# A second block of 128 tokens per expert, computed inside the expert loop

## The chip, the cores and the metric

The kernel runs on one core of one Trainium2 chip. The metric is the device time of one execution in microseconds (us). TensorE (PE) multiplies, and its weight loads (PEld) overlap its matmuls; VectorE (DVE), ScalarE (ACT) and GpSimd (POOL) do the element work; SyncE (SP) issues most DMA transfers. Every engine works through its own instruction stream and waits for the others on semaphores.

## What the reference computes

Six 128-row tiles of tokens (256 context, 512 latent) pass a first block of two layers and a second block of two layers. Both layers of the first block end in a mixture of experts, and only this part is touched:

```python
def hier_moe(h, w_rg, b_rg, w_re, b_re, w_gate, w_up, w_down):
    ...                                  # group, then top 2 of its 8 experts: 2 experts and weights a token
    order = jnp.argsort(flat_e)          # (token, expert) pairs sorted by expert
    padded = ((counts + MOE_BLOCK - 1) // MOE_BLOCK) * MOE_BLOCK      # MOE_BLOCK = 128
    ...
    def run_block(args):
        xb, e = args
        return (jax.nn.silu(xb @ w_gate[e]) * (xb @ w_up[e])) @ w_down[e]
    ...
    return jnp.zeros((n, d), h.dtype).at[tok_sorted].add(y[dest] * w_sorted[:, None])
```

There are 32 experts a layer. gate and up are 1024 x 512, down is 512 x 1024, all fp32: 6 MB an expert. Layer 0 routes 768 tokens (1536 pairs), layer 1 routes 512 (1024 pairs). Evaluated on its inputs, the reference's router gives, in layer 0, more than 64 pairs to experts 8, 10, 11, 12, 13 and 14, and more than 128 to expert 14 alone (132). In layer 1 experts 28 (65) and 31 (83) exceed 64, and none exceeds 128.

## The kernel before, in words

`moe` runs one layer. `scores` has sorted the pairs: `tix` lists for every expert the rows of its first 128 tokens, `idx` and `wl` where their results go and by what factor. `experts` (L1332) loops over the 32 experts in Python, so the code is unrolled. In step e GpSimd gathers the tokens of expert e+2 (`ex_load`, L1260), SyncE issues the twelve 512 KB weight chunks of expert e+1 (`ex_load_w`, `wraw`, L144), and TensorE finishes gate and up for the first 64 tokens of expert e (`ex_in`, L1275), transposes the tokens of e+1 (`ex_x`, L1284) and starts expert e+1. The chunks lie in a ring of 32 buffers (4 + 28), 2 2/3 experts deep: a chunk of a later expert can be issued when the chunk that had its buffer is no longer read.

Then `ex_arms` (L1376) branches: every engine has loaded the row of token 64 into a register (`values_load`, L1359). If it is a token, `ex_rest` computes the second 64 tokens too and writes both halves out; else `ex_out` writes one half: transposes (L1308), a copy (L1309), the down product, the scaling on VectorE (L1319 in layer 0 alone, L1320) and a scatter into the DRAM table Y by GpSimd (L1321).

Behind the loop come the blocks past 128 tokens. `past` (L1181) makes their lists in three steps, `count`, `blocks` and `fill`, that run behind the steps of the first experts; the number of such blocks is the register `nov`. If `nov > 0`, the weights of the first overflow expert are loaded again (`overflow`, L1139) and `ex_block` (L1146) computes it; a loop under `nov > 1` (L1149) does any further ones. Between the loop and this block `gains` spreads rows for the next stage (L441, L442). The next stage reads Y back (`load`, L52 after inlining into the pinned section) and warms TensorE up with a few matmuls.

The order of instructions on each engine is chosen by a planner that simulates the program; what goes through `keep_in_program_order` keeps its place among such instructions. The same planner spreads DMAs over eight completion counters shared by SyncE's and ScalarE's transfers; a DMA waits until the one before it on its counter is complete, whichever engine issued it.

Of the kernel before, what the change touches and what calls it, by code (L numbers as in the profile page):

```python
# [8 lines left out]
F32 = mybir.dt.float32  # L9
F32R = mybir.dt.float32r  # L10
BF = mybir.dt.bfloat16
# [21 lines left out]
NEG = -1.0e30  # L33
NOB = 12
RING = 4
MRING = 28
# [30 lines left out]
class Ker:  # L67
# [518 lines left out]
    def mixer_ab(self, xO, begin=None):  # L586
# [8 lines left out]
        with ExitStack() as eo:  # L595
# [260 lines left out]
            with ExitStack() as e1:  # L856
                pp = e1.enter_context(self.pool(name="abp", bufs=1))
                ps = e1.enter_context(self.pool(name="abps6", bufs=3, space=PSUM))
                self.weights(e1, 8, 0, "right")
                G = []  # L860

                def loads():
                    for t in (0, 1):
                        nc.sync.dma_start(xO[:, t, :], xsrc(t))
                    G.append(self.mod_rows(pp, 0, 1, 2, "gc", eng=nc.sync))
                    G.append(self.mod_rows(pp, 0, 0, 2, "gl", eng=nc.sync))
                    for t in range(2, NT):
# [213 lines left out]
    def moe(self, l, xO, t0, nt, who_of, sc=None, then=()):  # L1081
# [12 lines left out]
        with ExitStack() as e1:  # L1094
# [5 lines left out]
            off = pw.tile([P, 1], F32, name="off")  # L1100
            ctx = None if l else pw.tile([P, 2, NE + NOB], F32, name="ctx")
            for h in range(2):
                nc.gpsimd.memset(off[h * 64:h * 64 + 64], 2 * BIG + h)
# [6 lines left out]
            px = e1.enter_context(self.pool(name=f"mx{l}", bufs=2, side="right"))  # L1110
            ps = e1.enter_context(self.pool(name=f"mqs{l}", bufs=8, space=PSUM))
            xg = [pg.tile([P, D], F32, name=f"xg{i}", tag=f"xg{i}") for i in range(3)]
# [10 lines left out]
            past = self.past(nt, sc["K"], idx, tix, wl, eid, px, ps, off, ctx)  # L1123

# [10 lines left out]
            def overflow():  # L1135
# [3 lines left out]
                with tc.If(nov > 0):  # L1139
# [3 lines left out]
                return nov, w  # L1143
            nov, w = self.experts(l, tix, idx, wl, ctx, xg, hD, Y, T, px, ps,
                                  [first] + past + ([] if l else [self.shift_scale]), gains, overflow)
            with tc.If(nov > 0):  # L1146
                self.ex_block(w, xo, slots, px, ps, nc.values_load(tix[64:65, NE:NE + 1], min_val=0, max_val=int(BIG)))
            self.n = RING + 11
            with tc.If(nov > 1):  # L1149
# [30 lines left out]

    def past(self, nt, K, idx, tix, wl, eid, px, ps, off, ctx):  # L1181

# [6 lines left out]
        t_ = {}  # L1189

        def count():
            t_["iota"], t_["tri"] = self.const("iota128", [P, P], px), self.const("tri", [P, P], px)
            tri = t_["tri"]
# [5 lines left out]
            nb, nbi = T2("nb", 1, F32, NE), T2("nbi", 1, I32, NE)  # L1199
            v.tensor_scalar(nb, cn[:NE, 0:1], float(P - 1), None, ALU.add)  # L1200
            v.tensor_copy(nbi, nb)
# [10 lines left out]
        def blocks():  # L1212
# [10 lines left out]
            v.tensor_scalar(eid[:, :NOB], ef, float(NE - 1), None, ALU.min)  # L1223
            v.tensor_copy(eid[:, NOB:NOB + 1], ov[:, 2 * NE - 1:2 * NE])
            for k in range(2):
                tmp = px.tile([P, nt, NE], F32, name="ptmp", tag="ptmp", bufs=1)
# [3 lines left out]
                hi, bl, rm, neg = (T2(f"{n}{k}", nt) for n in ("hi", "bl", "rm", "ng"))  # L1230
                v.tensor_scalar(hi, K["r"][:, k], float(-P), None, ALU.add)
                ii = T2(f"ii{k}", nt, I32)
# [14 lines left out]
        def fill():  # L1247
# [28 lines left out]

    def ex_x(self, xg, px, ps):

        x = px.tile([P, 8, P], F32, name="xT", tag="xT")
        for g in range(2):  # L1280
# [20 lines left out]
    def ex_out(self, w, sg, h, idx, wl, Y, T, px, ps):  # L1301
# [29 lines left out]

    def experts(self, l, tix, idx, wl, ctx, xg, hD, Y, T, px, ps, past, gains, overflow):  # L1332

# [4 lines left out]
        w = self.ex_load_w(l, 0)  # L1338
        a = ps.tile([P, 512], F32, name="ea", tag="b")
        self.ex_in(a, w, x, 0, range(2))  # L1340
        for e in range(NE):
            if e + 2 <= NE:
                self.ex_load(tix[:, e + 2:e + 3], xg[(e + 2) % 3], hD, T)
# [11 lines left out]
            if e + 1 < NE:  # L1355
                a = ps.tile([P, 512], F32, name="ea", tag="b")
# [8 lines left out]
    def ex_block(self, w, xg, out, px, ps, more=None):  # L1365

        x = self.ex_x(xg, px, ps)
# [30 lines left out]
    def table(self, fn):  # L1398

        t = self.sm.tile([P, 1], F32, name="tab")  # L1400
        self.nc.scalar.activation(t, self.eps[EPS], fn)
# [9 lines left out]
    def mixer_na(self, xO, begin=None, finish=None):  # L1411
# [13 lines left out]
        with ExitStack() as e1:  # L1425
# [3 lines left out]
            with ExitStack() as e2:  # L1429
# [23 lines left out]
                with ExitStack() as e3:  # L1453
# [4 lines left out]
                    with self.pinned():  # L1458
# [32 lines left out]
                        for t in range(NT + 2):  # L1491
# [245 lines left out]
    def even_mixer(self, xO, normed=False, finish=None):  # L1737
# [3 lines left out]
        with ExitStack() as e1:  # L1741
            OT = xO[:, 4:6, :].rearrange("p a (b n) -> p (a b) n", n=512)
            with ExitStack() as e2:
# [8 lines left out]
                with ExitStack() as e3:  # L1752
# [46 lines left out]
                    else:  # L1799
# [148 lines left out]
    def conv_ffn(self, l, xO, dst=None):  # L1948
        nc, tc, I = self.nc, self.tc, self.I
        wu, wd = I["ffn_w_up_2"][l], I["ffn_w_down_2"][l]  # L1950
        with ExitStack() as e1:
            ph = e1.enter_context(self.pool(name=f"ff{l}", bufs=1))
            ps = self.banks()
# [361 lines left out]
```

## Time and profile before

| what | us |
| --- | --- |
| median of 3 runs (lowest, highest) | 3520.12 (3518.69, 3525.53) |
| the profiled execution | 3519.27 |
| its span, first to last instruction | 3517.5 |
| TensorE busy in the span | 3270.0 (93%) |
| VectorE, ScalarE, GpSimd busy | 1515.1, 1027.7, 468.3 |

The expert loop of layer 0 lies at about 611 to 1172 us of the span, its overflow block at 1175 to 1193, and the loop of layer 1 at about 1644 to 2165. A busy TensorE is an engine with an instruction in it; it does not say that the rest of the kernel waits for it.

### The profile page before, as it was taken

Reading aid. Unit: us, or ns where it says so; the run is one execution under the profiler, and the core shown is the slowest. Engines: PE = TensorE matmul, PEld = TensorE weight load, DVE = VectorE, ACT = ScalarE, POOL = GpSimd, SP = SyncE. Lnnn points to the kernel's source line nnn. Section 1 sums busy time; section 2 is a strip of 40 time slices with the busy share of each in tenths; the row PEclk is TensorE's granted clock in tenths of the full one; section 3 lists DMA queues with packets and bytes.
Section 4 is the critical chain, followed back from the end, with each engine's and each line's share of the span. In section 5 each row is a group of like instructions: output and inputs, shape, how many; then the busy total and the mean of one; then the engine's idle time right before and its main releaser. Section 6 shows DMA issues by size and latency. Waiting matters only on the chain. (4 is left out here: it accounts for less than half of the span.)

```text
span 3517.5 us, 44393 instructions
## 1 busy us (share of the span) xinstructions
PE 3270.0 (93%) x16460; PEld 2118.1 (60%) x16460; DVE 1515.1 (43%) x2899; ACT 1027.7 (29%) x1908; POOL 468.3 (13%) x569
## 2 busy tenths in 40 slices
PE   7999998999988699998988888998999999999998
PEld 5954556333322387765332234876888888788887
DVE  3476565222222356565211114527443456455344
ACT  3475541100000144441000002326332334333232
POOL 1044421111111023331111110103000000000000
PEclk9999999999999899999999999999999999999999
DMA  5134465798999622236999996322333354233331
GB/s 202 49 119 133 166 217 196 306 417 329 352 410 397 229 73 75 69 113 226 416 408 399 402 397 244 122 91 85 96 96 96 84 66 95 70 99 105 96 97 48
DMA packets 350859, 676.34 MB, mean 192 GB/s; under 512 B 42804, under 2 KB 194548, under 8 KB 349184
## 3 DMA queue, kind: packets, MB, share of 16 engines
q1 hardware_dynamic: 313816, 626.50, 50.6%
q0 software_dynamic: 17360, 25.94, 2.1%
q10 hardware_dynamic: 19416, 20.34, 1.8%
q8 instruction: 168, 2.75, 0.3%
q14 instruction: 99, 0.81, 0.1%
HBM read 676.22 MB, written 29.19 MB: 201 GB/s over the span
## 5 line engine op out<-in xcount | busy, mean ns | idle before, releaser
L1275 PE MATMUL ea<-wr,xT 128*64 128x512 f32 x2336 | 607.5, 601 | 38.5 <-DMA wr<-in_moe_w_up_dram 21.8
L157 DVE TENSOR_TENSOR wh<-wr,wh 128x1024 fp32r<-128x1024 f32 (+2 forms) x269 | 328.8, 1228 | 308.9 <-ACT wh L156 308.2
L240 PE MATMUL aw<-hh,wh 128*128 128x512 f32 (+1 forms) x1184 | 432.1, 366 | 2.9 <-ACT wh L156 2.6
L241 PE MATMUL aw<-hl,wh 128*128 128x512 f32 (+1 forms) x1184 | 432.7, 366 | 0.0
L242 PE MATMUL aw<-hh,wh 128*128 128x512 f32 (+1 forms) x1184 | 431.4, 365 | 0.0
L1275 PEld LDWEIGHTS ea<-wr,xT 128*64 128x64 f32 x2336 | 178.9, 137 | 408.9 <-issue 293.5
L156 ACT CAST wh<-wr 128x1024 fp32r<-128x1024 f32 (+2 forms) x269 | 274.2, 1027 | 417.6 <-PE acc L242 287.4
L1275 PE MATMUL ea<-wr,aT 128*64 128x512 f32 x1168 | 284.4, 632 | 53.0 <-DVE aT L1309 43.5
L240 PEld LDWEIGHTS aw<-hh,wh 128*128 128x128 f32 x1184 | 223.9, 189 | 39.7 <-ACT wh L156 3.5
L241 PEld LDWEIGHTS aw<-hl,wh 128*128 128x128 f32 x1184 | 224.3, 189 | 38.3 <-issue 3.5
L242 PEld LDWEIGHTS aw<-hh,wh 128*128 128x128 f32 x1184 | 224.1, 189 | 37.6 <-issue 3.5
L510 POOL TENSOR_TENSOR pp<-pp,rc 128x768 f32<-128x768 f32 (+3 forms) x192 | 211.0, 1106 | 260.0 <-DVE rc L509 247.3
L1285 ACT COPY xT<-pt 128x512 f32<-128x512 f32 x65 | 38.1, 586 | 683.8 <-PE pt L1284 672.9
L1275 PEld LDWEIGHTS ea<-wr,aT 128*64 128x64 f32 x1168 | 82.7, 144 | 200.1 <-issue 136.6
L1321 POOL DMA_INDIRECT Y<-ey,idx x73 | 73.1, 1001 | 848.3 <-DVE ey L1320 767.2
L508 ACT ACTIVATE pp<-s,nm 128x768 f32<-128x768 f32 (+3 forms) x192 | 137.1, 716 | 157.4 <-DVE nm L1593 81.1
L240 PE MATMUL acc<-wh,hh 128*128 128x512 f32 (+2 forms) x480 | 177.8, 370 | 0.0
L241 PE MATMUL acc<-wh,hh 128*128 128x512 f32 (+2 forms) x480 | 176.4, 368 | 0.0
L242 PE MATMUL acc<-wh,hl 128*128 128x512 f32 (+2 forms) x480 | 176.1, 367 | 0.0
L1297 ACT ACTIVATE sg<-ea 64x256 f32<-64x256 f32 x146 | 54.9, 376 | 302.4 <-PE ea L1275 237.7
L241 PE MATMUL acc<-wh,ah 128*128 128x512 f32 x352 | 137.8, 392 | 0.0
L1298 DVE TENSOR_TENSOR sg<-sg,ea 64x256 f32<-64x256 f32 x146 | 62.0, 425 | 175.7 <-ACT sg L1297 173.0
(493 smaller groups left out, 5166.5 us busy)
## 6 DMA issues: line engine op xcount, KB each, us to landing
wr<-in_moe_w_gate_dram SPq DMA_DIRECT2D x260, 512.0 KB
wr<-in_moe_w_up_dram SPq DMA_DIRECT2D x260, 512.0 KB
wr<-in_moe_w_down_dram SPq DMA_DIRECT2D x260, 512.0 KB
wr<-in_w_ada_dram SPq DMA_DIRECT2D x96, 512.0 KB
wr<-in_ffn_w_up_dram SPq DMA_DIRECT2D x88, 512.0 KB
wr<-in_ffn_w_down_dram SPq DMA_DIRECT2D x44, 512.0 KB
wr<-in_odd_w_in_dram SPq DMA_DIRECT2D x32, 512.0 KB
wr<-in_na_w_in_dram SPq DMA_DIRECT2D x30, 512.0 KB
```

Source lines behind the costliest of these rows:

```text
L156: keep(self.nc.scalar.copy(hi, raw))
L157: keep((self.lo_eng or self.nc.vector).tensor_sub(lo, raw, f(hi)))
L240: mm(ps, ah, bh, start=first, stop=False)
L241: mm(ps, ah, bl, start=False, stop=False)
L242: mm(ps, al, bh, start=False, stop=last)
L508: nc.scalar.activation(p[:, :n], s[:, b:b + n], AF.Exp, bias=nm, scale=sign, accum_out=rc)
L510: nc.gpsimd.tensor_mul(p[:, :n], p[:, :n], rc.broadcast_to([P, n]))
L1275: self.tc.keep_in_program_order(self.nc.tensor.matmul(*a, **k))
L1285: (self.nc.vector.tensor_copy if g else self.nc.scalar.copy)(x[:, g * 4:g * 4 + 4, :], pt.rearrange("p (k t) -> p k t", t=P))
L1297: self.nc.scalar.activation(sg[64:, c], a[:64, c], AF.Silu)
L1298: self.nc.vector.tensor_mul(sg[64:, c], sg[64:, c], a[64:, c])
L1321: nc.gpsimd.indirect_dma_start(Y.rearrange("t (h d) -> (t h) d", h=2), bass.IndirectOffsetOnAxis(ap=idx[:, h], axis=0), y, None, bounds_ch ...
```

## The change

Experts 3 to 31 (`TWO = 3`) get a second block of up to 128 tokens in the loop, from the weights that are still loaded: behind the arms of expert e stands a branch on the first row of its second list; in it are a gather, `ex_block` with all its arms, and the scatters. A new step `second` of `past`, at expert 1, makes the lists for it; `count`, `blocks`, `fill` move one expert later and count only what exceeds 256 tokens (128 for experts 0 to 2). Both branch registers are loaded at the head of each step. `gains` moves behind the first overflow block. `ea`, the product that is started early, has two PSUM banks of its own, the rest six. L1319 keeps its program order. Two `warm` calls read another tile (one has 9 matmuls for 6), and small unused tiles (`pad`) shift SBUF addresses.

```diff
+TWO = 3
@@ mixer_ab, mixer_na, conv_ffn
+                self.pad(e1, 192, "right")
...
+                self.pad(e2, 352, "right")
...
+                self.pad(e1, 192)
@@ past
+        def second():
+            t_["iota"], t_["tri"] = self.const("iota128", [P, P], px), self.const("tri", [P, P], px)
+            so, sw = (ps.tile([P, 512], F32, name=n, tag="b")[:, :NE] for n in ("so2", "sw2"))
+            for k in range(2):
+                rm = T2(f"rm{k}", nt)
+                v.tensor_scalar(rm, K["r"][:, k], float(-P), None, ALU.add)
+                R2 = px.tile([P, nt, P], BF, name="R2", tag=f"R2{k}", bufs=1)
+                self.ranked(R2, rm, t_["iota"])
+                for acc, val in ((so, K["aid"]), (sw, K["wp"])):
+                    self.lists(acc, R2, self.marks(px, K["E"][:, k], val[:, k]), k == 0, k == 1)
+            self.places(so, two["tix"])
+            for dst, acc, o in ((two["idx"], so, off), (two["wl"], sw, None)):
+                t = T2("ovs2", NE)
+                v.tensor_copy(t, acc)
+                self.both(dst, t, ps, o, two["ctx"] if o is not None else None)
...
-        return [count, blocks, fill]
+        return [second, count, blocks, fill]
@@ ex_out
-            nc.vector.scalar_tensor_tensor(y, self.dgain, ctx[:, h], self.gain, ALU.mult, ALU.add)
+            self.tc.keep_in_program_order(
+                nc.vector.scalar_tensor_tensor(y, self.dgain, ctx[:, h], self.gain, ALU.mult, ALU.add))
@@ experts
         for e in range(NE):
+            more = nc.values_load(tix[64:65, e:e + 1], min_val=0, max_val=int(BIG))
+            if e >= TWO:
+                tok = two["tix"][:, e:e + 1]
+                more2 = nc.values_load(tok[0:1], min_val=0, max_val=int(BIG))
...
-            more = nc.values_load(tix[64:65, e:e + 1], min_val=0, max_val=int(BIG))
+
+            def second():
+                with self.tc.If(more2 < T):
+                    self.ex_load(tok, xg[e % 3], hD, T)
+                    at = [q if q is None else q[:, :, e:e + 1] for q in (two["idx"], two["wl"], two["ctx"])]
+                    self.ex_block(w, xg[e % 3], (at[0], at[1:], Y, T, px, ps), px, ps,
+                                  nc.values_load(tok[64:65], min_val=0, max_val=int(BIG)), x)
             self.ex_arms(more, w, x, sg, out, px, ps)
+            if e >= TWO:
+                second()
             w, x = w1, x1
-        gains()
@@ moe
-            ps = e1.enter_context(self.pool(name=f"mqs{l}", bufs=8, space=PSUM))
+            ps = e1.enter_context(self.pool(name=f"mqs{l}", bufs=6, space=PSUM))
...
             with tc.If(nov > 0):
                 self.ex_block(w, xo, slots, px, ps, nc.values_load(tix[64:65, NE:NE + 1], min_val=0, max_val=int(BIG)))
+            gains()
@@ mixer_na, even_mixer
-                                self.warm(ps, xO[:, 0, 0:512], 6)
+                                self.warm(ps, A[0][:, 0:512], 6)
...
-                        self.warm(ps, xO[:, 2, 0:512], 6)
+                        self.warm(ps, self.gfin[:, 0:512], 9)
```

## Rows read from the trace of the kernel before

**Rows 1.** Busy us (count) of each engine by stretch, then granted clock, DMA share, GB/s.

```profile
820.00:920.00 100.00, 94.23 (x462) 33.32 (x459) 24.59 (x45) 8.36 (x20) 12.04 (x12) 1.00 0.83 292
920.00:1150.00 230.00, 208.47 (x884) 69.64 (x882) 51.31 (x89) 20.08 (x45) 28.31 (x28) 1.00 1.02 405
1650.00:1660.00 10.00, 9.41 (x72) 4.90 (x72) 2.38 (x6) 3.21 (x5) 1.00 (x1) 1.00 0.08 14
1840.00:2130.00 290.00, 254.98 (x1066) 87.78 (x1064) 47.38 (x88) 23.51 (x53) 33.44 (x33) 0.96 1.02 401
```

**Rows 2.** What SyncE waited for, 600 to 700 us: total us, times, longest.

```profile
SPq L144 <- PE pt L1308: 21.5, 3, 15.9
SPq L144 <- DMA c_aid<-const_aid_dram: 16.2, 1, 16.2
```

**Rows 3.** The same, 820 to 920 us: all of its answer.

```profile
SPq L144 <- PE ea L1275: 62.3, 26, 9.4
SPq L144 <- PE pt L1308: 9.0, 3, 8.0
```

**Rows 4.** Timeline of TensorE: transposes for experts 15 to 17, a down product between.

```profile
882.66 1.09 PE L1284 MATMUL pt<-c_ident,xg 128*128 128x128 f32 x8
906.97 1.09 PE L1284 MATMUL pt<-c_ident,xg 128*128 128x128 f32 x8
...
915.99 3.65 PE L1275 MATMUL ea<-wr,aT 128*64 128x512 f32 x16 [0.52 <-DVE aT L1309]
...
919.58 1.09 PE L1284 MATMUL pt<-c_ident,xg 128*128 128x128 f32 x8
```

**Rows 5.** The same in layer 1, two light experts that follow each other.

```profile
1740.37 1.09 PE L1284 MATMUL pt<-c_ident,xg 128*128 128x128 f32 x8
1754.77 1.09 PE L1284 MATMUL pt<-c_ident,xg 128*128 128x128 f32 x8
```

**Rows 6.** Timeline behind expert 14's last product: VectorE's scaling, GpSimd's scatter and gather.

```profile
907.09 0.75 DVE L1320 SCALAR_TENSOR_TENSOR ey<-ea,wl,ey 128x512 f32<-128x512 f32 x1 [3.76 <-PE ea L1275]
...
908.12 0.96 POOL L1321 DMA_INDIRECT Y<-ey,idx  x1 [3.85 <-DVE ey L1320]
909.39 1.04 POOL L1260 DMA_INDIRECT xg<-hD,tix  x1 [0.30 <-issue]
```

**Rows 7.** Line L1260, all gathers of the kernel: issue to landing.

```profile
DMA to landing us min/median/max: 3.2/7.1/9.1
```

**Rows 8.** Timeline of layer 0's end: expert 31's last product, then the overflow block.

```profile
1165.32 0.75 DVE L1319 SCALAR_TENSOR_TENSOR ey<-dgain,ctx,gain 128x512 f32<-128x512 f32 x1 [5.48 <-DMA Y<-ey,idx]
...
1166.63 5.00 PE L1275 MATMUL ea<-wr,aT 128*64 128x512 f32 x16 [6.40 <-issue]
...
1171.67 0.75 DVE L1320 SCALAR_TENSOR_TENSOR ey<-ea,wl,ey 128x512 f32<-128x512 f32 x1 [5.14 <-PE ea L1275]
...
1175.33 1.09 PE L1284 MATMUL pt<-c_ident,xg 128*128 128x128 f32 x8
...
1187.11 5.00 PE L1275 MATMUL ea<-wr,aT 128*64 128x512 f32 x16 [1.17 <-DVE aT L1309]
...
1192.17 0.75 DVE L1320 SCALAR_TENSOR_TENSOR ey<-ea,wl,ey 128x512 f32<-128x512 f32 x1 [5.11 <-PE ea L1275]
```

**Rows 9.** Timeline of layer 1's end: the matmuls of `gains`, before an overflow branch not entered.

```profile
2164.26 2.05 PE L441 MATMUL mrow<-gsrc,c_ident 16*128 16x128 f32 x16
```

**Rows 10.** Sequencer instructions of three branch lines and the register load: ns min/median/max.

```profile
L1146 PEldq EVENT_SEMAPHORE  x2: 51/51/51, 2166.3 to 2166.5; - x2
L1149 PEldq COMPARE_BRANCH  x2: 329/892/1454, 1187.4 to 2166.7; - x2
L1376 PEldq COMPARE_BRANCH  x74: 70/234/3554, 625.2 to 2160.7; - x74
L1359 PEldq TENSOR_LOAD <-tix x64: 295/303/493, 624.6 to 2144.9; - x64
```

**Rows 11.** Groups by line, 590 to 700 us: list matmuls of 32 columns, rank comparison.

```profile
L1058 PE MATMUL swp<-Wm,Rm 128*128 128x32 bf16 x36 | 1.2, 176 | 0.0
L1050 DVE TENSOR_TENSOR R<-c_iota,rm 128x768 bf16<-128x768 f32 x2 | 1.9, 950 | 0.0
```

More of the change, by code (lines that the diff above doesn't have):

```diff
@@ L1101, in moe @@
             ctx = None if l else pw.tile([P, 2, NE + NOB], F32, name="ctx")
+            two = dict(tix=pw.tile([P, NE], I32, name="tix2"), idx=pw.tile([P, 2, NE], I32, name="idx2"),
+                       wl=pw.tile([P, 2, NE], F32, name="wl2"), ctx=None if l else pw.tile([P, 2, NE], F32, name="ctx2"))
             for h in range(2):
@@ L1122, in gains @@
                     self.nA = {w: self.spread(pg, self.nmod[0], 16 * w + 8, ps, f"xg{i}") for i, w in enumerate(ws)}
-            past = self.past(nt, sc["K"], idx, tix, wl, eid, px, ps, off, ctx)
+            past = self.past(nt, sc["K"], idx, tix, wl, eid, px, ps, off, ctx, two)
             def first():
@@ L1143, in overflow @@
                 return nov, w
-            nov, w = self.experts(l, tix, idx, wl, ctx, xg, hD, Y, T, px, ps,
-                                  [first] + past + ([] if l else [self.shift_scale]), gains, overflow)
+            nov, w = self.experts(l, tix, idx, wl, ctx, two, xg, hD, Y, T, px, ps,
+                                  [first] + past + ([] if l else [self.shift_scale]), overflow)
             with tc.If(nov > 0):
                 self.ex_block(w, xo, slots, px, ps, nc.values_load(tix[64:65, NE:NE + 1], min_val=0, max_val=int(BIG)))
+            gains()
             self.n = RING + 11
@@ L1179, in moe, with past @@
         return finish
-    def past(self, nt, K, idx, tix, wl, eid, px, ps, off, ctx):
+    def past(self, nt, K, idx, tix, wl, eid, px, ps, off, ctx, two):
         nc = self.nc
@@ L1189, in past @@
         t_ = {}
+        def second():
[13 more added lines that the diff above has]
+                self.both(dst, t, ps, o, two["ctx"] if o is not None else None)
         def count():
-            t_["iota"], t_["tri"] = self.const("iota128", [P, P], px), self.const("tri", [P, P], px)
             tri = t_["tri"]
@@ L1199, in count @@
             nb, nbi = T2("nb", 1, F32, NE), T2("nbi", 1, I32, NE)
-            v.tensor_scalar(nb, cn[:NE, 0:1], float(P - 1), None, ALU.add)
+            v.reduce_sum(nb, self.ident[:NE, TWO:NE], axis=AX.X)
+            v.scalar_tensor_tensor(nb, nb, float(-P), cn[:NE, 0:1], ALU.mult, ALU.add)
+            v.tensor_scalar(nb, nb, float(P - 1), None, ALU.add)
             v.tensor_copy(nbi, nb)
@@ L1224, in blocks @@
             v.tensor_copy(eid[:, NOB:NOB + 1], ov[:, 2 * NE - 1:2 * NE])
+            late = T2("late", NE)
+            v.tensor_scalar(late, t_["iota"][:, :NE], float(TWO), None, ALU.is_ge)
             for k in range(2):
+                tmp = px.tile([P, nt, NE], F32, name="ptmp", tag="ptmp", bufs=1)
+                hi, bl, rm, neg = (T2(f"{n}{k}", nt) for n in ("hi", "bl", "rm", "ng"))
+                v.tensor_mul(tmp, K["E"][:, k], late.unsqueeze(1).broadcast_to([P, nt, NE]))
+                v.reduce_sum(hi, tmp, axis=AX.X)
+                v.tensor_scalar(hi, hi, 1.0, float(-P), ALU.add, ALU.mult)
+                v.tensor_add(hi, hi, K["r"][:, k])
                 tmp = px.tile([P, nt, NE], F32, name="ptmp", tag="ptmp", bufs=1)
@@ L1229, in blocks @@
                 v.reduce_sum(og, tmp, axis=AX.X)
-                hi, bl, rm, neg = (T2(f"{n}{k}", nt) for n in ("hi", "bl", "rm", "ng"))
-                v.tensor_scalar(hi, K["r"][:, k], float(-P), None, ALU.add)
                 ii = T2(f"ii{k}", nt, I32)
@@ L1275, in mmo, with ex_x @@
         self.tc.keep_in_program_order(self.nc.tensor.matmul(*a, **k))
-    def ex_x(self, xg, px, ps):
-        x = px.tile([P, 8, P], F32, name="xT", tag="xT")
+    def ex_x(self, xg, px, ps, x=None):
+        if x is None:
+            x = px.tile([P, 8, P], F32, name="xT", tag="xT")
         for g in range(2):
@@ L1330, in ex_rest, with experts @@
         self.ex_out(w, sg2, 1, *out)
-    def experts(self, l, tix, idx, wl, ctx, xg, hD, Y, T, px, ps, past, gains, overflow):
+    def experts(self, l, tix, idx, wl, ctx, two, xg, hD, Y, T, px, ps, past, overflow):
         nc = self.nc
@@ L1338, in experts @@
         w = self.ex_load_w(l, 0)
-        a = ps.tile([P, 512], F32, name="ea", tag="b")
+        a = ps.tile([P, 512], F32, name="ea", tag="ea", bufs=2)
         self.ex_in(a, w, x, 0, range(2))
         for e in range(NE):
+            more = nc.values_load(tix[64:65, e:e + 1], min_val=0, max_val=int(BIG))
+            if e >= TWO:
+                tok = two["tix"][:, e:e + 1]
+                more2 = nc.values_load(tok[0:1], min_val=0, max_val=int(BIG))
             if e + 2 <= NE:
@@ L1355, in experts, with ex_block @@
             if e + 1 < NE:
-                a = ps.tile([P, 512], F32, name="ea", tag="b")
+                a = ps.tile([P, 512], F32, name="ea", tag="ea", bufs=2)
                 self.ex_in(a, w1, x1, 0, range(2))
             out = idx[:, :, e:e + 1], (wl[:, :, e:e + 1], None if l else ctx[:, :, e:e + 1]), Y, T, px, ps
-            more = nc.values_load(tix[64:65, e:e + 1], min_val=0, max_val=int(BIG))
+            def second():
[4 more added lines that the diff above has]
+                                  nc.values_load(tok[64:65], min_val=0, max_val=int(BIG)), x)
             self.ex_arms(more, w, x, sg, out, px, ps)
+            if e >= TWO:
+                second()
             w, x = w1, x1
-        gains()
         return over
-    def ex_block(self, w, xg, out, px, ps, more=None):
-        x = self.ex_x(xg, px, ps)
+    def ex_block(self, w, xg, out, px, ps, more=None, x=None):
+        x = self.ex_x(xg, px, ps, x)
         a = ps.tile([P, 512], F32, name="ea", tag="b")
@@ L1398, in table @@
     def table(self, fn):
-        t = self.sm.tile([P, 1], F32, name="tab")
+        t = self.sm.tile([P, 1], F32, name="ss")
         self.nc.scalar.activation(t, self.eps[EPS], fn)
@@ L1951, in conv_ffn @@
         with ExitStack() as e1:
+            if l:
+                self.pad(e1, 192)
             ph = e1.enter_context(self.pool(name=f"ff{l}", bufs=1))
```

## The prediction

> **What bounds the kernel now.** I read the granted clock of the core first (0.977 in the mean, one core, so no neighbour to compare), then the page's slices to find the two expert loops, then busy time by stretch, then what SyncE waited for, and the timeline at the places that the diff touches.
>
> TensorE is busy 93% of the span, but in the expert loops it shares the lead with the weight stream. Layer 0 has two kinds of stretch. From 820 to 920 us the DMA engines are only 0.83 busy at 292 GB/s [rows 1], and every one of SyncE's waits there is for TensorE, 62.3 + 9.0 us of 100 [rows 3]: the ring is full, and the stream stands until TensorE lets go of a buffer. These are the heavy experts 8 and 10 to 14: one takes 24.31 us between two groups of transposes, a light one 12.61 [rows 4]. From 920 to 1150 us the DMA share is 1.02 at 405 GB/s [rows 1]: the stream leads, and what TensorE does more than now costs nothing while a step stays under the stream's 16.4 us or so (14 steps in 230 us). Layer 1 is of this second kind from its first experts on: 1.02 and 401 GB/s from 1840 to 2130 [rows 1]. A stream that has stood still does not catch up, so time lost for it early is lost at the end. It stands at each layer's start: share 0.08 from 1650 to 1660 [rows 1], and in layer 0 SyncE waits 21.5 us for experts 0 and 1 and 16.2 us for a small constant `c_aid` that ScalarE issues late [rows 2].
>
> So each edit is judged by where it falls: at the start, 1:1; in 820 to 920, 1:1; where the stream leads, nothing; behind the last weights, 1:1.
>
> **The lists at expert 1 (added).** 60 list matmuls of 32 columns: 36 such take 1.2 us [rows 11], so 2.0, and 16 small fp32 matmuls for `both`, under 1; on VectorE two rank comparisons of 0.95 [rows 11] and the marks, an estimated 5 us in sum, mostly beside gate and up of experts 1 and 2. `count`, `blocks` and `fill` move one expert on, at the same price. The trace has no list step at expert 1. Low end 1 us a layer (in TensorE's idle time), high end 12 (VectorE's 5, TensorE's 3, and 4 if `tix2` comes late and SyncE, which now loads the branch register before issuing expert 4, stops for it). I take 4 a layer, nearer to the matmuls' own row, since the marks have gate and up beside them: +8.
>
> **The branch that is not taken (added, 57 of 58 times).** TensorE must run empty before it raises its semaphores for the skipped code. The trace has this once, at an `ex_block` that is skipped: its last matmul ends at 2164.26 + 2.05 = 2166.31 [rows 9], the two semaphore steps run to 2166.5, and the next sequencer instruction is at 2166.7 [rows 10]: 0.4 us. Matmuls overlap (16 in 3.65 us [rows 4], 0.6 each), so an empty array loses another 0.37. The two register loads of 0.30 each [rows 10] now stand at the head of the step, where no queue hides them if the planner leaves them there. Bounds 0.4 and 1.8 (all, and a branch of 0.35); I take 1.2. In the stretch that TensorE leads, experts 8 to 13 and 15 pay: 7 x 1.2 = +8.4. Behind layer 0's last weights two pay (+2.4); at layer 1's end, where heavy expert 28 has put TensorE behind, four (+4.8). Everywhere else the stream covers it: 12.6 + 1.2, and 14.4 + 1.2 in layer 1 [rows 5], are under 16.4. GpSimd's skip (a counter step and two loads) delays the next gather as well; a gather is issued at 909.4 for transposes at 919.6 [rows 4, 6] and lands in 7.1 [rows 7], so 3 us are to spare. SyncE and ScalarE pay under 1 us a step and lead nothing.
>
> **The branch that is taken: expert 14 of layer 0.** Its block is in series, inside the stretch that TensorE leads, and holds the ring: nothing of expert 14's weights is free before it has read them. First the gather, issued in the branch behind the last scatter: GpSimd's order is scatter at 908.12, then a gather at 909.39 [rows 6], 2.4 us behind the product's end at about 907.0; it lands 3.2 to 9.1 us later [rows 7], and since the stream stands I take 5: TensorE idles 7.4 us. Then the block itself, which the trace has as today's overflow block: from 1175.33 to 1187.11 + 5.00 = 1192.11 [rows 8], 16.8 us. Sum +24.2; bounds 21 (landing 3.2, and a faster down product) and 29 (landing 9.1, and 2 for a clock that falls in the idle time).
>
> **The overflow block that goes.** With expert 14 done in the loop `nov` is 0 in both layers. The last scaling moves from 1192.17 to where expert 31's now is, 1171.67 [rows 8]: -20.5. `gains` was in that stretch; behind the branch it runs beside the scatter and the read of Y, so nothing. The reloaded weights of 6 MB go too, but the block waited for none of them.
>
> **L1319 kept in order.** At 1165.32 it sits on VectorE ahead of the copy that TensorE needs, waiting for a scatter, and the down product waits 6.40 us [rows 8]. Behind the product it would be the scaling that waits: from 1171.67 to about 1166.1, -5.6. At most that, at least 0 (if the planner keeps today's order); the code asks for just this, so I take it.
>
> **The rest.** Six shared PSUM banks in place of eight, the pads, the other warm sources: no wait on a bank or for such a tile stands on the chain today; bounds -3 and +3, value 0. The 9 matmuls for 6 run while Y is read.
>
> **Sum.** Layer 0: 4 + 8.4 + 24.2 + 2.4 - 20.5 - 5.6 = +12.9. Layer 1: 4 + 4.8 = +8.8. Together +21.7 on the profiled execution's 3519.3 (span 3517.5 and 1.8 around it), 3541.0; that execution lies 0.85 below the median, so I state 3542. Low ends (lists 1 + 1, skips 13 x 0.4, block 21, -26.1, -3) give -1, 3519; high ends (12 + 12, 13 x 1.8, 29, -20.5, +3) give +59, 3579.
>
> **The rivals.** *The false wait goes.* Place: SyncE at expert 4 of layer 0, behind `c_aid`, 16.2 us [rows 2], while the stream stands. `c_aid` can only be overwritten when the last marks have read it, and these move one expert later; the planner may then put it on a counter that the stream meets later, when enough is in flight. Then layer 0 starts up to 16.2 us earlier and, the stream being the leader up to expert 8, keeps it: 3542 - 16 = 3526, not slower; with cheap lists and skips 3503 or so. It decides from a wait under some 4 us. Against it: the marks and the loads behind them move together, and the wait can as well come back, one expert on.
>
> *Code is not there when the branch jumps.* Half of the arms' 74 branches take under 0.234 us, but one took 3.554 and one of the two skips at L1149 took 1.454 [rows 10]. The skipped code is longer than that of the arms: 112 matmuls of an expert with both halves, as many weight loads, and the light arm's. If each skip cost 3.3 in place of 1.2: 7 x 2.1 = 15 in layer 0, and in layer 1 a step of 14.4 + 3.3 = 17.7 against 16.4, some 28 steps, 36: 3542 + 51 = 3593. For it: these two rows. Against it: the skip of the very `ex_block` at 2164 cost 0.4. [...]
>
> *It doesn't do what it says:* the 4 tokens still go to the overflow block (a limit off by one in the new counts). Then +4 + 8.4 + 8.4 + 2.4 + 4.8 in lists and skips, -5.6: about 3541, with a block behind the loop still to be seen.
>
> **How the numbers follow.** Forecast 0.62, false wait gone 0.23, code 0.11, not done 0.04. The likeliest's own range is 3519 to 3579. To leave out at most 2 in 10 the range takes the false wait's cases down to 3506 and most of the code's up to 3590. Within 0.2% (7 us, about what a measurement of this kernel can tell from no change) is 3513 to 3527: faster 0.13 from the false wait and 0.04 from the forecast's low end; same 0.06 + 0.07; slower the rest, 0.70.
>
> **What would show it.** The transposes of experts 15 and 16 stand about 49 us apart in place of 24.3, with a gather and an `ex_block` between them and SyncE waiting for TensorE throughout. Light experts behind heavy ones are 13.8 apart, not 12.6. No block follows expert 31 in layer 0; from its last scaling to the read of Y it is under 6 us. The DMA share at each layer's start shows 4 us more of standing. I am wrong if light experts keep 12.6 (skips are free), if the stretch of expert 14 grows by under 20, if `c_aid` holds nobody, or if branches of 1 us and more appear on TensorE at each expert.

## Result: 3603.5 us, 2.3% slower

The changed kernel takes 3603.5 us (median of 4, 3597.3 to 3605.6) beside 3520.6 for the kernel before (3518.7 to 3525.5): ratio 1.0231, 95% interval [1.0219, 1.0243]. The forecast was 3542 and its range ended at 3590: the direction was right, the size was not. The profiled execution has a span of 3603.8 us at a mean granted clock of 0.964.

Where the 86 us between the two spans lie, read from the transposes with which each expert starts (us):

| stretch | before | after | difference |
|---|---|---|---|
| start to expert 0 of layer 0 | 611.4 | 608.3 | -3.1 |
| expert 0 to 31, layer 0 | 527.1 | 596.2 | +69.1 |
| expert 31 of layer 0 to expert 0 of layer 1 | 505.8 | 482.5 | -23.3 |
| expert 0 to 31, layer 1 | 488.4 | 524.2 | +35.8 |
| expert 31 of layer 1 to the end | 1384.8 | 1392.6 | +7.8 |

The passage behind layer 0's loop came as forecast in sum (-26.1 and +2.4 make -23.7). The two loops did not: +36.6 for the first and +8.8 for the second with the tail had been expected.

### The profile page after: what moved, and what is told of

The parts are those of the page before. It is cut to its first block, busy times and chain, and to the rows that moved or that the text cites. A ratio compares the mean times of both kernels' runs of the same rounds, so it can differ in the third digit from the quotient of the medians.

```text
span 3603.8 us, 46176 instructions
## 1 busy us (share of the span) xinstructions
PE 3300.0 (92%) x16598; PEld 2156.0 (60%) x16598; DVE 1527.9 (42%) x2942; ACT 1029.1 (29%) x1910; POOL 472.6 (13%) x574
## 5 line engine op out<-in xcount | busy, mean ns | idle before, releaser
L1304 PE MATMUL ea<-wr,xT 128*64 128x512 f32 x2336 | 584.0, 604 | 17.2 <-PEq L1397 16.5
L157 ACT CAST wh<-wr 128x1024 fp32r<-128x1024 f32 (+2 forms) x269 | 274.1, 1027 | 417.9 <-PE acc L243 285.0
L1304 PE MATMUL ea<-wr,aT 128*64 128x512 f32 x1168 | 327.3, 711 | 49.2 <-ACTq L1397 28.3
L1304 PEld LDWEIGHTS ea<-wr,aT 128*64 128x64 f32 x1168 | 105.2, 162 | 216.8 <-issue 159.1
L1315 DVE COPY xT<-pt 128x512 f32<-128x512 f32 x65 | 44.9, 691 | 344.1 <-PE pt L1314 344.1
```

The costliest lines, as they stand in the source:

```text
L157: keep(self.nc.scalar.copy(hi, raw))
L1304: self.tc.keep_in_program_order(self.nc.tensor.matmul(*a, **k))
L1315: (self.nc.vector.tensor_copy if g else self.nc.scalar.copy)(x[:, g * 4:g * 4 + 4, :], pt.rearrange("p (k t) -> p k t", t=P))
```

## The profile after

Busy time by stretch, as in [rows 1]:

```profile
820.00:920.00 100.00, 93.05 (x436) 34.63 (x434) 23.52 (x43) 8.34 (x20) 12.03 (x12) 1.00 0.75 281
960.00:1150.00 190.00, 160.97 (x655) 59.38 (x656) 38.13 (x66) 14.69 (x33) 22.29 (x22) 0.91 0.99 376
1790.00:2000.00 210.00, 173.86 (x776) 68.53 (x774) 34.77 (x65) 17.37 (x39) 27.03 (x27) 0.93 1.02 400
2000.00:2200.00 200.00, 170.47 (x724) 63.67 (x720) 32.62 (x61) 15.82 (x36) 23.27 (x23) 0.94 0.98 378
```

The line to look at is the second. Before, the rest of layer 0's loop ran at 405 GB/s with the clock at 1.00; now 376 GB/s and 0.91, though no expert there takes its second block. The share of 0.99 hides this; the rate does not. The stream has lost its lead, as SyncE's waits from 940 to 1200 us say:

```profile
SPq L145 <- PEq L1397: 89.6, 14, 13.8
SPq L145 <- DMA wr<-in_moe_w_down_dram: 37.5, 39, 1.9
```

L1397 is the new branch. In this stretch SyncE should only be held by its own transfers in flight ("DMA wr"); instead it stands 89.6 us for TensorE to come past a branch, because a weight buffer of an expert is given back only there. So TensorE leads, and its step must be read. One light expert that skips its second block, TensorE alone:

```profile
1015.26 1.09 PE L1314 MATMUL pt<-c_ident,xg 128*128 128x128 f32 x8
1016.29 2.80 PE L1304 MATMUL ea<-wr,xT 128*64 128x512 f32 x12
1020.11 0.30 PE L1338 MATMUL pt<-c_ident,sg 64*128 64x64 f32 x2 [1.02 <-DVE sg L1328]
1020.88 0.33 PE L1338 MATMUL pt<-c_ident,sg 64*128 64x64 f32 x2 [0.47 <-DVE sg L1328]
1021.85 5.35 PE L1304 MATMUL ea<-wr,aT 128*64 128x512 f32 x16 [0.64 <-ACTq L1397]
1027.00 4.46 PE L1304 MATMUL ea<-wr,xT 128*64 128x512 f32 x18
1031.81 1.04 PE L1304 MATMUL ea<-wr,xT 128*64 128x512 f32 x2 [0.35 <-PEq L1397]
1032.78 1.09 PE L1314 MATMUL pt<-c_ident,xg 128*128 128x128 f32 x8
```

The same place in the step of 12.61 us before, between the transposes and the down product of [rows 4]:

```profile
908.00 7.09 PE L1275 MATMUL ea<-wr,xT 128*64 128x512 f32 x32
915.01 0.46 PE L1308 MATMUL pt<-c_ident,sg 64*128 64x64 f32 x4
```

A record is one instruction in the trace; a product of 512 columns leaves two. Three things differ:

- *Order.* Of the 32 gate and up records only 12 stand ahead of the light arm; the 20 of the next expert, which before all ran there and covered the activation, come behind the down product. TensorE idles 1.02 and 0.47 us for `sg`. This makes 14.4 us, the step that layer 1 had before [rows 5].
- *Clock.* The down product takes 5.35 us for 3.65 [rows 4]: 8 to 10 of its 16 records last 0.8 to 1.1 us in place of 0.59. They come behind that idle time, at a granted clock of 0.50 (1022.8 to 1025.5 us; 1.00 from 1027 to 1031). From expert 0 to 31, records of 128x512 above 0.7 us number 164 in layer 0 and 177 in layer 1, 51 and 50 before. The granted clock (the third number from the end) is 0.90 in this step and 1.00 in a later one of 15.8 us without such records (busy time of TensorE alone):

```profile
1015.26:1032.78 17.52, 15.04 (x61) 0.90 1.01 371
1102.18:1117.95 15.77, 13.33 (x61) 1.00 1.01 377
```

- *Emptying.* TensorE idles 0.35 us ahead of the last two records, for the skipped branch, and these take 1.04 us by themselves (18 in a row take 4.46). In all the branch costs some 1.4, as steps at full clock show: heavy ones 25.74 for 24.31, a light one 15.78 for 14.41 (run 1).

14.4 + 1.4 is 15.8, still under the stream's 16.4; with the clock it is 17.4, over it. The branch itself can be long:

```profile
L1397 PEldq COMPARE_BRANCH  x58: 78/428/6120, 681.5 to 2244.8; - x58
```

23 of the 58 take over 1 us (1.6 to 6.1), 92 us beyond 0.4 each in sum; [rows 10] had one such in 74. But the sequencer is ahead of the products: the branch of this step stands at 1026.16 us, before the 18 records that begin at 1027.00 and take 4.46 us, and heavy steps are 25.74 with a branch of 0.33 as with one of 3.54. Most of it is hidden, not all.

Expert 14's block, with the transposes of 15, of the block and of 16 (the timeline of all engines):

```profile
901.39 1.09 PE L1314 MATMUL pt<-c_ident,xg 128*128 128x128 f32 x8
...
922.67 0.97 POOL L1352 DMA_INDIRECT Y<-ey,idx  x1 [3.93 <-DVE ey L1351]
923.97 1.04 POOL L1289 DMA_INDIRECT xg<-hD,tix  x1 [0.34 <-issue]
926.90 1.06 PE L1314 MATMUL pt<-c_ident,xg 128*128 128x128 f32 x8 [1.04 <-DMA xg<-hD,tix]
...
943.85 1.09 PE L1314 MATMUL pt<-c_ident,xg 128*128 128x128 f32 x8
```

The gather is issued 2.4 us behind the product, as in [rows 6], but TensorE idles only 1.04 us for it: the next expert's 18 records, now behind the arms, fill the wait. 42.5 us from expert 15 to 16, against 24.3 before: the block costs 18.2 (16.7 beside a heavy step of after, which has a skip in its place).

The false wait of [rows 2] is still there, one expert later and longer (600 to 720 us):

```profile
SPq L145 <- DMA c_aid<-const_aid_dram: 20.7, 1, 20.7
```

And the end of layer 0, which answers [rows 8]: no overflow block, `gains` (L442) behind the branch.

```profile
1220.70 3.62 PE L1304 MATMUL ea<-wr,xT 128*64 128x512 f32 x14 [0.30 <-PEq L1397]
...
1227.67 5.29 PE L1304 MATMUL ea<-wr,aT 128*64 128x512 f32 x16 [1.22 <-ACTq L1150]
1234.69 4.31 PE L442 MATMUL mrow<-nA,c_ident 32*128 32x128 f32 x32 [1.74 <-DVEq L1150]
```

## Experiments

Medians and ratios are against the kernel before, run on the same chip (3520.2, 3521.6 and 3522.8 us in the three groups of four). "Loops" gives expert 0 to 31 of layer 0 and of layer 1; before 527.1 and 488.4, after 596.2 and 524.2.

**1. The second block behind expert 14 alone.** No other expert of this input needs one.

```
-            if e >= TWO:
+            if e == 14:
                 second()
```

> The changed kernel (3603.5 us), but the second block stands only behind expert 14 of each layer, so 56 of the 58 branches are gone; lists, six banks and handover stay. My theory, from the trace of after: the loss sits in TensorE's step of a light expert, which is 17.4 us in layer 0 (12.6 before) because the array is emptied at each skipped branch, the next expert's first products stand behind the arms and the clock then falls in the gap. Without the branches the light step is under the stream's 16.4 again, and layer 0 gives back 30 to 40, layer 1 some 15: 3553 (3540 to 3565). Rival 'lists': the loss is made at the start of each layer (8 to 10 us behind in layer 0, 24 in layer 1 by expert 38) and in the longer hold of the weights' buffers; then the branches give back under 20: 3585 or more. Rival 'code is fetched': the 30 long branches go, up to 107 us of branch time beyond 0.4 us each: 3520 or below.

3526.9 us, ratio 1.0014 [1.0004, 1.0023]; loops 556.1 and 494.3. Fifty-six branches that are never taken cost 76.6 us. Light steps alternate between 14.41 and 16.11, one at full clock and the next with 8 to 10 slow records: the order and the clock are disturbed here too, but both steps stay under the stream's 16.4 and cost nothing. Heavy steps are 24.40, so 1.35 is the branch's own part. The time lies below my range (3540 to 3565). The rival 'lists' is out; 'code is fetched' fits the size, not yet the cause.

**2. Order pinned.** An ordering edge from the arms' first transposition to the next expert's fourth gate and up product.

```
+            if k == 0 and self.cover is not None:
+                self.tc.add_manual_dep(t.ins, self.cover.ins.name, ...)
```

> The changed kernel with one order pinned: the next expert's first four gate and up products (8 records on TensorE) stand ahead of the arms in both layers, as they stood in layer 0 of the kernel before, so that TensorE has work while the activation runs. All 58 branches stay. My theory (order and clock): a light step falls from 17.4 to about 13.8 where TensorE leads, the slow down products (1.06 us a matmul for 0.59) go, and the stream leads again from about expert 21 of layer 0: minus 25 to 35 in layer 0, minus 8 to 14 in layer 1, 3562 (3555 to 3580). Rival 'emptying': the branch itself, not the order, makes the step long; the light step stays over 16.4 and the time within 8 us of 3603. Rival 'code is fetched': no change either, since the same code is skipped.

3556.9 us, 1.0099 [1.0082, 1.0116]; loops 567.7 and 509.5: 46.6 us come back with all 58 branches in place. A light step is 13.23, a heavy one 24.83 (0.52 for the branch), slow records fall to 70 and 117. SyncE's waits, 940 to 1200 us:

```profile
SPq L145 <- DMA wr<-in_moe_w_up_dram: 47.6, 52, 2.0
...
SPq L145 <- PEq L1403: 11.0, 7, 8.5
```

11.0 us for the branch (here L1403) in place of 89.6: the stream leads again. Both rivals had said no change.

**3. A shorter second block.** Only a light expert's code: no arms inside, no second half (expert 14's 4 tokens fit the first).

```
-                    self.ex_block(w, xg[e % 3], ..., x)
+                    self.ex_x(xg[e % 3], px, ps, x)
+                    b = ps.tile([P, 512], F32, name="ea", tag="b")
+                    self.ex_in(b, w, x, 0, range(8))
+                    self.ex_out(w, self.ex_act(b, px), 0, at[0], at[1:], Y, T, px, ps)
```

> The changed kernel, but the second block holds a light expert's code only (no arms inside, half 0 alone; expert 14's 4 tokens of this input fit): the skipped code on TensorE falls from 48 to 36 kept calls less the two inner arms, that is from 88 calls to 36. Rival 'code is fetched': branches of 2.4 to 6 us at the skip (23 of 58, 92 us in sum beyond 0.4 each) shrink or go, and the time falls by 20 to 60: 3545 to 3583. My theory: these long branches lie behind some 18 queued products (4.5 us) and cost nearly nothing (heavy steps are 25.74 with a branch of 0.3 as with one of 3.5); then the time stays within 8 us of 3603, with shorter branches in the trace.

3587.0 us, 1.0184 [1.0166, 1.0202]; loops 589.0 and 510.2.

```profile
L1397 PEldq COMPARE_BRANCH  x59: 78/335/1458, 683.2 to 2224.8; - x59
```

One long branch is left of 23, so here the long branches come with the long skipped code. What else comes with them stands in after's trace, in the packets of q8, the queue that the page calls "instruction": in each of the 23 long branches a packet of 16384 B lands 1.3 to 1.6 us before the branch ends, and in none of the 35 others. That these packets carry the code behind the jump is my reading; the trace has their queue, size and time alone. Run 12 has the same in all of its 57 long branches. In before, one lands 1.35 and 1.53 us ahead of the end of the two branches over 1 us (3.55 at L1376, 1.45 at L1149, [rows 10]). The transfers during one of after's longest branches, 1146.66 to 1152.78 us, have one:

```profile
q8 instruction: 1, 0.02, 1.1%
```

The time falls by 16.5: more than my "nothing", less than the rival's 20 to 60. Light steps keep 17.3.

**4. Lists and small edits without any second block.** The second lists are computed and not used; the old counts, so the overflow block is back.

```
-            if e >= TWO:
-                second()
-            v.reduce_sum(nb, self.ident[:NE, TWO:NE], axis=AX.X)
...
+            v.tensor_scalar(nb, cn[:NE, 0:1], float(P - 1), None, ALU.add)
```

> The changed kernel without any second block and with the old counts, so that the overflow block takes expert 14's 4 tokens as before: what is left of the change is the second lists at expert 1 (computed, not used), six banks for eight, the moved handover, the pads and L1319 kept in order. My theory: second lists plus 8 a layer as the step behind expert 2 grew (22.7 for 13.9 in layer 0, 21.7 for 13.9 in layer 1), some of it given back by the stream in layer 0, L1319 minus 5.6: 3530 (3523 to 3540). Rival 'nothing but branches': 3515 (before, less 5.6). Rival 'lists and hold': the whole start loss of layer 1 (24) and layer 0 (10) is there: 3545 or more.

3513.3 us, 0.998 [0.997, 0.999], below the forecast's range and where the rival 'nothing but branches' had it (3515). The lists cost 3.1 us from expert 0 to 9 of layer 0 and 6.3 from 0 to 7 of layer 1, but the end of layer 0 gives back 16.5 (489.3 for 505.8). Against run 1 (+13.6) this prices expert 14's block less the overflow block. Light steps are 14.41 and 16.11 here as well, though `more` alone is loaded early: the order is lost without any second branch.

**5. L1319 kept in order, alone, on the kernel before.**

```
-            nc.vector.scalar_tensor_tensor(y, self.dgain, ctx[:, h], self.gain, ALU.mult, ALU.add)
+            self.tc.keep_in_program_order(
+                nc.vector.scalar_tensor_tensor(y, self.dgain, ctx[:, h], self.gain, ALU.mult, ALU.add))
```

> The kernel before with the one line L1319 kept in order, nothing else of the change. The prediction's step: minus 5.6 at the end of layer 0, 3514.6; the run with the lists only came out at 3513 with a last step of layer 0 that was 12.6 shorter (24.2 for 36.8), so up to minus 13: 3507 to 3515. Rival: the down product's 6.40 us of waiting turns into another wait of the same length (for the scatter, or the gather of the overflow block), 3519 to 3521.

3513.7 us, 0.9978 [0.9969, 0.9988]. Its end of layer 0:

```profile
1158.12 5.35 PE L1275 MATMUL ea<-wr,aT 128*64 128x512 f32 x16 [0.63 <-issue]
...
1163.40 3.83 PE L441 MATMUL mrow<-nA,c_ident 32*128 32x128 f32 x32
1167.17 1.09 PE L1284 MATMUL pt<-c_ident,xg 128*128 128x128 f32 x8
```

The wait of 6.40 us in [rows 8] is 0.63. And one sees what stands between the last product and the overflow block: `gains`, 3.8 us.

**6. A dummy product in the gap.**

```
         with many.Else():
+            self.warm(ps, w[0][0][0][:, 0, :], 1)
             self.ex_out(w, sg, 0, *out)
```

> The changed kernel with one dummy fp32 product of 128x512 (two records, about 0.9 us) on TensorE in the light arm, ahead of the activation's transposes, where TensorE now idles 1.03 us; nothing is left out. Theory 'clock': it is this idle time behind which the down product runs at the lower clock (8 to 10 of its records at 0.8 to 1.1 us for 0.59, some 1.7 us a step); filled, the light step falls from 17.4 to 15.8, under the stream's 16.4: 3565 (3555 to 3585). Rival 'lateness alone': the clock falls as often, the dummy product only adds: 3603 or more, light steps 17.4 or longer.

3576.2 us, 1.0152 [1.0132, 1.0173]; loops 573.9 and 517.4. Work was added and 27.4 us were gained. A light step:

```profile
1038.06 2.80 PE L1304 MATMUL ea<-wr,xT 128*64 128x512 f32 x12
1040.79 1.12 PE L233 MATMUL warm<-wr,c_ident 128*128 128x512 f32 x2
1041.88 0.30 PE L1338 MATMUL pt<-c_ident,sg 64*128 64x64 f32 x2
1042.65 0.33 PE L1338 MATMUL pt<-c_ident,sg 64*128 64x64 f32 x2 [0.47 <-DVE sg L1328]
1043.63 3.65 PE L1304 MATMUL ea<-wr,aT 128*64 128x512 f32 x16 [0.64 <-ACTq L1397]
```

The idle 1.02 is filled and the down product is back at 3.65; slow records fall from 164 and 177 to 55 and 63. The step is 15.0, 2.4 less: 1.7 of it is the down product, the rest is that all 20 records of the next expert now stand in one row ahead of the skip, not 18 and 2 on its two sides. So the 27.4 us are the clock's in the main, not alone. The clock theory holds (granted clock 0.99 from 960 to 1150 us for 0.91); the idle times of 0.47 and 0.64 that remain did not bring the slow records back.

**7. Runs 2 and 3 together.**

```
+                self.tc.add_manual_dep(t.ins, self.cover.ins.name, ...)
...
-                    self.ex_block(w, xg[e % 3], ..., x)
+                    self.ex_out(w, self.ex_act(b, px), 0, at[0], at[1:], Y, T, px, ps)
```

> Order pinned (as in the run with the cover, 3556.9) and the short second block (as in the half body, which alone gave 16.5). Theory 'code fetch counts where few products are queued ahead of the branch': with the order pinned only 6 products (2.6 us) stand ahead of a branch of up to 6 us, so its 25 long branches (96 us beyond 0.4 each) cost more than before the pinning; without them 3532 (3522 to 3540), and the irregular steps of layer 1 (13.2 to 19.8 us) become even. Rival: the half body's gain was made where TensorE waited at the light arms only, which the pinning already covers: 3548 or more.

3551.8 us, 1.0083 [1.0067, 1.0098]; loops 563.2 and 502.7. Only 5 below the pinned order: the rival was right, what the short block gains lies mostly where the pinned order gains too. So order, clock and the shorter skipped code together take back 51.7 us of the loss (6 of the 59 branches are still over 1 us); the other 25 that run 1 does not have stay.

**8. The kernel before, with L1319 kept and the order pinned.**

```
+            self.tc.keep_in_program_order(
+                nc.vector.scalar_tensor_tensor(y, self.dgain, ctx[:, h], self.gain, ALU.mult, ALU.add))
...
+                self.tc.add_manual_dep(t.ins, self.cover.ins.name, ...)
```

> The kernel before with L1319 kept in order and the next expert's first four gate and up products pinned ahead of the arms in both layers (they were so in layer 0, and only late in layer 1); no second lists, no second blocks. Theory: TensorE's light step of layer 1 falls from 14.4 to 12.6, but the stream leads there, so this gives at most the few steps behind heavy ones and the start: 3508 (3502 to 3514). Rival: a wash or a loss, since products pinned ahead wait for their weights with the arms queued behind them: 3515 or more.

3511.6 us, 0.997 [0.9958, 0.9982], the same as run 5 (3513.7): here, where the stream leads, TensorE's order was worth nothing.

**9. Run 5 with `gains` moved behind the overflow block.**

```
             w, x = w1, x1
-        gains()
         return over
...
                 self.ex_block(w, xo, slots, px, ps, ...)
+            gains()
```

> The kernel before with L1319 kept in order (3513.7 by itself) and the handover spreads moved behind the overflow block, as the change has them; no second lists, no second blocks. Theory: the spreads stood on TensorE between the last expert and the overflow block; the run with the lists only, which has them moved, has a last step of layer 0 of 24.2 us where L1319 alone has 31.3, so minus 7: 3507 (3503 to 3511). Rival: they only change places, and what they cost is then paid behind the block, while Y is read: 3512 to 3516.

3508.7 us, 0.9958 [0.9944, 0.9972]: some 5 more than L1319 alone, though the two intervals touch. It has the lowest median here and is faster than both kernels by more than the noise, with nothing of the second block in it.

**10. Run 1 with the order pinned.**

```
-            if e >= TWO:
+            if e == 14:
                 second()
...
+                self.tc.add_manual_dep(t.ins, self.cover.ins.name, ...)
```

> The second block only behind expert 14 (3526.9) with the order pinned (the cover). This is the surrounding that the prediction had assumed for the branches: light step 12.6 where TensorE leads. Against it the run with the cover and all 58 branches (3556.9) gives the price of 56 skips where the order is not lost. Theory: the order alone gives little without the branches, since 14.4 and 16.1 are under the stream's 16.4 as well: 3522 (3515 to 3528), so 56 skips cost some 35. Rival: the order is worth as much here as with the branches (46): 3490 or less, more than the lists-only run leaves room for.

3543.3 us, 1.0061 [1.0045, 1.0076]: 16 us slower than run 1 (14 when each is taken against its own group's kernel before), which neither theory had. Without branches to cover, the pinned order makes the transposes wait for the copy of `xT` (0.7 us at 23 of the experts between 1760 and 2150 us) and later for weights (21 and 9 us there for gate and up). So the pin is no gain in itself. Run 7, with 56 skips more, is 8.5 us slower; that is no clean price for them, since run 10's own steps are longer (light 13.65 for 13.07, heavy 25.26 for 24.68).

**11. The two register loads back ahead of the arms.**

```
         for e in range(NE):
-            more = nc.values_load(tix[64:65, e:e + 1], min_val=0, max_val=int(BIG))
-            if e >= TWO: ... more2 = ...
...
+            more = ...; more2 = ...
             self.ex_arms(more, w, x, sg, out, px, ps)
```

> The changed kernel with one part undone: the two register loads (more, more2) stand directly ahead of the arms again, not at the head of the step. The planner then puts the next expert's first products ahead of the arms in layer 0, as before the change. Theory: the moved loads are what lost the order, and with it the cover and the clock: 3557 (3548 to 3570), as the run with the cover. Rival: the second branch behind the arms is what costs, wherever the loads stand: 3595 or more.

3588.4 us, 1.0196 [1.018, 1.0212]; loops 586.4 and 515.9. The time misses both ranges; the mechanism is half a hit. Order and clock came back with these lines: light steps of 14.00, 63 and 54 slow records. So the early loads let the planner put the arms first. But now one product of two records (1.02 us) stands between arms and second branch, and the long branches are exposed:

```profile
L1393 PEldq COMPARE_BRANCH  x58: 78/2140/6082, 683.0 to 2225.8; - x58
```

41 of 58 above 1 us, 122 us beyond 0.4 each; heavy experts beside such a branch take 31.3 and 29.7 for 25.7. The skipped code is as long as in after, so how many branches are long went with what stands ahead of them too.

**12. The second block's code twice in the branch.** Expert 14's tokens are computed twice.

```
+                    for _ in range(2):
                         self.ex_block(w, xg[e % 3], ..., x)
```

> The changed kernel with the second block's body written twice in a row inside the branch (expert 14 of layer 0 computes its 4 tokens twice, some 17 us more; the same rows are written). The skipped code is twice as long. Theory 'code is fetched': the share of long branches rises with the length of what is jumped over (1 of 59 with the half body, 23 of 58 with the whole one), to most of 58, and the time by 17 plus 10 to 40: 3630 to 3660. Rival: any jump past a certain length costs the same, as often as now (some 23 of 58): 3617 to 3625.

3662.2 us, 1.0408 [1.0388, 1.0427]; loops 615.8 and 548.7.

```profile
L1397 PEldq COMPARE_BRANCH  x58: 78/6014/7397, 682.8 to 2300.2; - x58
```

57 of 58 are long, 296 us beyond 0.4 each. The time is 2 us over the forecast's end. The second pass costs 15.6 (58.1 from expert 15 to 16 for 42.5); the other 43 of the 58.6 us come with the longer skip. With the same order the length of the skipped code made the difference in these three runs: 1 of 59, 23 of 58, 57 of 58.

## Why the prediction failed, step by step

**One term carries the miss.** The forecast put 13 skipped branches at 1.2 us, 15.6 in all, and the other 44 at nothing. Run 1 measures 56 of the 57 at 76.6. The difference, 61.0, is the miss (61.5). Without the skips the sum of the other terms was 3526.4; run 1 came out at 3526.9. That they agree to half a microsecond is luck, as the terms below were off by up to 10 us each way.

**The step that failed** is "Everywhere else the stream covers it", with 12.6 + 1.2 and 14.4 + 1.2 under 16.4. The price of a skip was right: 1.35 on heavy experts, bounds 0.4 to 1.8. The step to which it was added was not 12.6. The diff moves the register load to the head of the step. I charged it 0.30 us as an instruction and did not ask what it does to the planner, to whom the arms now seemed ready first. That took the cover off the activation (14.4), slow records behind the idle time made it 16.1 (run 1), and 1.35 more came out at 17.4, over 16.4: the light steps from expert 16 to 31 of layer 0 are 17.4 in the mean (15.8 to 19.1). In layer 1 the 14.4 was in the forecast; there the sum lacked the clock. Runs 2, 6 and 11 each take one link out. This and the shorter skipped code account for 51.7 of the 76.6 us (run 7).

**"Light experts behind heavy ones are 13.8 apart":** 17.4, for this reason; 13.2 with the order pinned.

**"Code is not there when the branch jumps"** was the rival nearest to the time (3593), and the text had listed its sign. It was there (23 branches over 1 us in after, each with a packet, as under run 3), with a price not of 3.3 a skip but of 16.5 in all (run 3), since most of a long branch lies behind queued products: a heavy step is 25.74 with a branch of 3.54 as with one of 0.33. In the trace a 512-column product leaves two weight loads and two matmuls and a transposition one of each; so the skipped code is an estimated 120, 264 and 528 instructions in runs 3, after and 12. By this length the long branches go from 1 of 59 over 23 of 58 to 57 of 58; at 264 run 11 has 41 of 58. Why one skip of 264 is long and the next is not, no run shows. What I argued against this rival, one cheap skip at 2164, was one case alone: after has 3.23 at the same branch. In the tail's 7.8 it is the smaller part: 4.7 lie ahead of the end of layer 1's last product, around the light arm of expert 30 (order, clock and skip again), and 2.6 between that end and the warm-up.

**The branch that is taken:** 18.2 for 24.2, under the 20 that the prediction had named as a sign of being wrong. The block was right (16.8 forecast, 17.0 from its transposes to those of expert 16); the 7.4 of idling for the gather was 1.04, as 18 records of the next expert fill it.

**The overflow block and L1319:** with two skips -23.7 forecast, -23.3 measured over the whole passage between the layers. The parts were not so good. Run 1, without the overflow block, is only 10.7 shorter there than run 4, which has it (478.6 for 489.3); the forecast was 20.5. L1319 gives 7.8 alone (run 5, forecast 5.6). `gains`, priced at nothing, was worth 5 (run 9): it stood on TensorE ahead of the overflow block, and that the read of Y would hide it was said of its new place only.

**The lists:** 9.4 for 8. **The false wait:** it came back one expert on, 20.7 us for 16.2, as the text had allowed.

What stays open: 25 of the 76.6 us remain with order, clock and long code taken back (run 7 against run 1). They can be the skips' own price, the pin's cost, or the weight buffers that are held until the second branch is past; no run changes that hold alone. Why the pinned order costs 16 us where no branch follows (run 10) was read from waits, not tried by itself.

## What to carry to other kernels

A step that is hidden has a margin (here 14.4 under 16.4), and every edit in it draws on the same margin: add up what an edit does to the order, to the idle time and, as here, to the slow records behind it (14.41 to 16.11 a step in run 1), before calling it covered. A register load that moves tells a planner that a branch is ready; look at the order of the instructions on each engine, not at the load's price. Keep the code that is jumped over short (worth 16.5 us here, run 3), and some microseconds of queued work ahead of the jump: behind 18 records (4.46 us) a heavy step was 25.74 with a long branch, behind one product (1.02 us, run 11) 31.3 and 29.7.

## What the runs showed of the hardware

- The branch that jumps over the second block (L1397) took TensorE's sequencer 0.1 to 1.0 us in after, or 1.6 to 6.1 where a packet on q8 landed in it (up to 7.4 in run 12). How often went with the length: over an estimated 120 instructions 1 of 59 were long (run 3), over 264 23 of 58 (after), over 528 57 of 58 (run 12). It went with what stands ahead as well: 6 of 59 at 120 (run 7), 41 of 58 at 264 (run 11). The size of a packet, in after:

```profile
q8 instruction: 232, 3.80, 0.4%
```

That is 16.4 KB a packet (before 168 and 2.75 MB, as large). There are more of them with more code in the branches: 172 in run 1, 199 in run 3, 232 in after, 277 in run 12.

- In light steps of after an idle time of 1.02 us ahead of a product was followed by 8 to 10 slow records (0.8 to 1.1 us for 0.59; the granted clock was 0.50 from 1022.8 to 1025.5 us), and one dummy product there removed most of them (164 and 177 slow records, then 55 and 63): most of 27 us, for work that nobody needs. It is no strict rule: in after's steps at 1051.1, 1154.1 and 1170.6 us the idle time was longer (3.2 us in the step for 2.4) and no record was slow, and in run 1 steps with the same 2.1 us of idle time come with and without slow records.
